# Attention scores of the last row group as three float32r products of split keys and queries

## The chip, the cores and the metric

The kernel runs on one NeuronCore of one Trainium2 chip. The metric is the device time of one execution in microseconds (us), as the median of several executions. A change of less than about 0.2% can hardly be told from none.

TensorE (PE) multiplies matrices and writes to the eight PSUM banks. VectorE (DVE), ScalarE (ACT) and GpSimd (POOL) do the elementwise work, each strictly in the order of its own list of instructions. SyncE (SP) issues nearly all DMAs, also in order. A weight load of PE is shown as a row of its own (PEld).

## The reference

One layer of a token mixer with 2-D neighbourhood attention, between two RMSNorms. x is 2048 tokens x 1024, seen as 32 rows of 64 columns; there are 16 heads of 64.

```
h = rmsnorm(x, norm_0)
q, k, v, gate = split(h @ w_in_0, 4)
# token (r, c) sees 8 rows and 16 columns of keys around it
s = q @ k.T / 8 + bias(rpb_0); s = -1e30 outside the neighbourhood
o = softmax(s) @ v
x = x + (o * silu(gate)) @ w_out_0
out = rmsnorm(x, norm_f)
```

Everything is float32, and the result is compared in float32.

## The kernel before

**Number formats.** A float32 matmul takes several passes over its data. The big products (projections, output projection) avoid them: each operand is split on arrival into a rounded part h and a rest l, both of type float32r, and the product is h·h + h·l + l·h, three matmuls of one pass each. The split is one copy on ACT (it rounds) and one subtraction on DVE. The attention's own products (scores, transposes, values) are plain float32 matmuls.

**Stages.** `stage_one` and `stage_two` compute most of q, k, v and gate and send them to DRAM. Then a loop of 33 iterations does the attention, and PE fills the time between its pieces with the rest of the projections and, later, with the output projection (lines L1346, L1348, L1350, tile `po`), which is handed out in portions by `feed`.

**Attention units.** A unit is a pair of heads p (0 to 7) and a row group T (0 to 3: eight rows of 64 queries each). `order` lists the 32 units: first all p with T = 0, then T = 1 and 2, and at the end, in iterations 24 to 31, all p with T = 3. For T = 3 there are 12 rows of keys, so a tile of keys has 12 x 64 = 768 columns. The two heads of a pair lie in partitions 0 to 63 and 64 to 127 of the tiles `kt` and `q`.

**One iteration m** issues, in this order:

- `begin(m)`: the DMAs for the gate tile `sgt` of unit m-1, the values of unit m, the queries and keys of unit m+1
- a portion of filling work, and then `normalise` of the probabilities of unit m-1 (L1046 and after): a reciprocal on DVE, scalings on POOL and ACT
- `run_roots` (L1248 to L1255: eight small DVE operations for the final norm of an output row block), `split_rows` (L1198, L1199: splits a block for the output projection), the rest of the portion; evacuations of finished `po` banks (L1231 on DVE, then a square on ACT, L1234) and scalings of finished rows (L1263, DVE) come up in between
- `turns(m-1)`: 44 transposes on PE into six banks `ph` (L1112), copied to `pta` by three copies on ACT and three on DVE (L1088)
- `scores(2m)`, `scores(2m+1)`: for each of four column blocks C and both heads s one matmul of 64 x 128 queries by the keys (L1027) into a bank of its own; DVE reads each bank, adds the mask and bias `em` and takes the row's extreme (L1035); ACT takes the exponential (L1041)
- `values(2m-2)`, `values(2m-1)`: matmuls into bank `o` (L1134), which DVE multiplies by `sgt` into `og` (L1140).

All eight PSUM banks are one pool. In an iteration six go to `ph`, eight to the scores, one to `o`, and one holds the unfinished `po`. So the scores take over the banks of `po` and `ph` in turn, each as soon as its copy is done, the last score bank waits for DVE's first read of a score of the same unit, and `o` waits for DVE's second read.

**Portions.** Iterations up to 24 get about 16 matmuls of filling each, iterations 25 to 31 get 53.

```
amount = [dense] * 25
...
amount += [(96 * (12 - len(units_two)) + 546 - sum(amount) - first - end_of_it) / (cycles - 25)] * (cycles - 25) + [end_of_it]
```

Of the kernel before, what the change touches and what calls it, by code (L numbers as in the profile page):

```python
# [10 lines left out]
F32 = mybir.dt.float32  # L11
F32R = mybir.dt.float32r
BF16 = mybir.dt.bfloat16
I32 = mybir.dt.int32
AF = mybir.ActivationFunctionType
OP = mybir.AluOpType
# [4 lines left out]
ROWS, GW, KH, KW = 32, 64, 8, 16  # L21
# [12 lines left out]
KEY_ROWS = [(0, 11), (4, 19), (12, 27), (20, 32)]  # L34
# [36 lines left out]
def build(ctx, tc, x, xr, xt, wg, rpb, last, w_out, n0, nf, masks, out):  # L71
    nc = tc.nc
# [8 lines left out]
    def pool(name, bufs):  # L81
        p = ctx.enter_context(tc.tile_pool(name=name, bufs=bufs))
        return lambda shape, dt, nm: p.tile(shape, dt, name=nm, tag=name)
# [3 lines left out]
    wp = pool("wp", 8)  # L87
    raw = pool("raw", 6)
    kp = pool("kp", 2)
    qp = pool("qp", 2)  # L90
    vp = pool("vp", 2)
    vhalf = []
# [4 lines left out]
            vhalf.extend((t[:, :512], t[:, 512:]))  # L97
        return vhalf.pop(0)

    sp = pool("sp", 2)  # L100
    xp = pool("xp", 8)
    mkp = pool("mkp", 1)
    pt = pool("pt", 1)
    mp = pool("mp", 10)
    ep = pool("ep", 2)

    def sixths():
        t = pt([128, 3072], F32R, "sixths")
        return [t[:, i * 512:i * 512 + 512] for i in range(6)]

    lp = pool("lp", 1)
# [5 lines left out]
    def bank(n, name):  # L117
        return banks.tile([128, n], F32, name=name, tag="bank")
# [138 lines left out]
    for n, (k, j, ph, c) in enumerate(halves):  # L257
        a = (KINDS[k] + j, ph)
# [79 lines left out]
    def must(*keys):  # L338
        assert all(k in written for k in keys), keys
        for n in range(len(later) - 1, -1, -1):  # L340
            if later[n][1] in keys:
                for _ in range(n + 1):
                    later.pop(0)[2]()
                break
# [225 lines left out]
    def stage_one():  # L570
# [6 lines left out]
        land["x12"] = [kp([128, 960], F32, "land")[:, :512] for _ in range(2)] + [xp([128, 512], F32, "land") for _ in range(2)]  # L577
        sixth = sixths()
        land["x21"] = [spot[:, k] for k in range(3)] + [lp([128, 512], F32, "land")]
        slots = [(mp, 512)] * 8 + [(sp, 512)] * 2 + sixth[:2] + [(vh, 512)] * 4  # L580
        slots += sixth[2:] + [(mp, 512)] * 2 + [(qp, 512)] * 2

        def load(f, k):
# [163 lines left out]
        for k in range(4):  # L747
            y = ev([128, 512], F32, "y")
            a, b, c = land["x11"][k], land["x12"][k], land["x22"][k]
# [48 lines left out]
    def stage_two():  # L798
        x12, x11, x21 = L2["x12"], L2["x11"], L2["x21"]
        x22 = [xp([128, 512], F32, "land") for _ in range(4)]  # L800
        sixth = sixths()
        for k in range(4):
            load_x(2, "x22", k, x22[k])
        slots = {"T2": [(mp, 512)] * 8,
                 "T3": [(sp, 512)] * 2 + sixth[:5] + [(lp, 512)],
                 "T4": [(vh, 512)] * 4 + [(mp, 512)] * 2 + [sixth[5], (qp, 512)]}

        def also(n, i):
# [120 lines left out]


    KT, VT, QT, EM, SG, E = {}, {}, {}, {}, {}, {}
    LAST, stored_at = {}, {}
    order = [(p, 0) for p in range(NP)] + [(p, T) for p in range(NP) for T in (1, 2)] + [(p, 3) for p in range(NP)]
    pairs = [(p, T, (h, h + 1)) for p, T in order for h in (0, 2)]
# [9 lines left out]
    def load_k(p, T):  # L944
        r0, r1 = KEY_ROWS[T]
        n = (r1 - r0) * GW
        must(*[("k", p, c) for c in range(r0 // 8, (r1 + 7) // 8)])

        def keys():
            t = kp([128, 960], F32, "kt")  # L950
            KT[p, T] = t.rearrange("p (r c) -> p r c", c=GW)
            nc.sync.dma_start(t[:, :n], kd[p][:, r0 * GW:r1 * GW])

        return keys

    def load_q(p, T):
        must(("q", p, T))
# [58 lines left out]
    def scores(i, between=None):  # L1016
        p, T, cs = pairs[i]
        kt, qt = KT[p, T], QT[p, T]
        r0, r1 = KEY_ROWS[T]
        got = []  # L1020
        for C in cs:
            c0, c1 = KEY_COLS[C]
            qs = slice(C * 128, C * 128 + 128)
            pst = [bank((r1 - r0) * (c1 - c0), f"s{s}") for s in range(2)]
            for s in range(2):
                a = slice(s * 64, s * 64 + 64)
                nc.tensor.matmul(pst[s], qt[a, qs], kt[a, :r1 - r0, c0:c1].rearrange("p r (s c) -> p s r c", c=8), start=True, stop=True)  # L1027
            got.append((C, pst))
        ST[i] = st = tiny.tile([128, 12], F32, name="st")
        for j, (C, pst) in enumerate(got):  # L1030
            n = (r1 - r0) * width(C)
            X[i, C] = [xp([128, 512], F32, f"x{s}")[:, :n] for s in range(2)]
            for s in range(2):
                o = 2 * j + s
                nc.vector.tensor_tensor_reduce(X[i, C][s], pst[s], EM[p, ROW_TYPE[T], COL_TYPE[C], s], -1.0, 1e38,  # L1035
                                               OP.add, OP.min, st[:, o:o + 1])
            if between and j == 0:
                between()
            for s in range(2):
                o = 2 * j + s  # L1040
                nc.scalar.activation(X[i, C][s], X[i, C][s], AF.Exp, bias=st[:, o:o + 1], scale=-1.0,  # L1041
                                     accum_out=st[:, 4 + o:5 + o])

    def normalise(i, both=False, between=None):
        st = ST.pop(i)
        nc.vector.reciprocal(st[:, 8:12], st[:, 4:8])  # L1046
        for j, C in enumerate(pairs[i][2]):
            if j and between:
                between()
            for s in range(2):  # L1050
                o = 8 + 2 * j + s
                if both and j:
                    nc.scalar.activation(X[i, C][s], X[i, C][s], AF.Copy, scale=st[:, o:o + 1])
                else:
                    nc.gpsimd.tensor_scalar(X[i, C][s], X[i, C][s], st[:, o:o + 1], 1.0, op0=OP.mult, op1=OP.mult)  # L1055
# [305 lines left out]
    cycles = len(order)  # L1361
# [14 lines left out]
    def feed(n, calm=0):  # L1376
        credit[0] += n
        while credit[0] > 0 or credit[0] > -calm_debt and clock[0] - state["event"] < calm:
            if alive[0]:
                got = next(fill, None)  # L1380
                if got is None:
                    alive[0] = False
                    continue
            else:
                got = next(outs, None)
                if got is None:
                    due(max(credit[0], 0.0))
                    credit[0] = min(credit[0], 0.0)
                    return
            credit[0] -= got  # L1390
            due(got)
# [37 lines left out]
    for m in range(cycles + 1):  # L1429
        a = amount[m] - 8  # L1430
        begin(m)
        feed(8)
        if m:
            due_here = []
            quiet[0] = True
            if a < 12 and m > 8 and m % 2:
                normalise(2 * m - 1, True, lambda: due_here.append(split_rows() or consume(1, turn=True)))
            else:
                normalise(2 * m - 1, True)
            if a > 12:  # L1440
                run_roots()
            elif not rows_due():
                run_roots(1)
            for k in range(3):
                if m == 1 and k == 2:
                    pass
                elif a > 12 or not any(due_here) and (k < 1 or k < 2 and m > 8 and m % 2 == 0):
                    got = split_rows()
                    due_here.append(got)
                    if not got:  # L1450
                        consume(1, turn=True)
                    elif a < 12 and m % 2 == 0 and len(items) - state["used"] == 8:
                        feed(a * 0.2)
                        consume(1, turn=True)
                feed(a * 0.2)
        else:
            feed(a * 0.6)
        quiet[0] = False
        feed(a * 0.4, 8 if a > 12 else 4)
        sums = next_sums(m) == m + 1  # L1460
        if m:
            turns(m - 1)
            first_sums = m + 2 if m + 2 in pair_steps else m + 1 if sums and m + 1 not in pair_steps else None
            if first_sums:
                after = tiny.tile([128, 12], F32, name="st")
                nc.gpsimd.tensor_scalar(after[:88, 0:1], PT[m - 1][:88, 1, 0:1], ones[:88, 0:1], 1.0, op0=OP.mult, op1=OP.mult)
                tables(first_sums, 0, 1)
        if m == cycles:
            all_loads()
            feed(6)  # L1470
        else:
            scores(2 * m)
            if sums:
                tables(m + 1, 2)
            if m == 0:
                feed(first)
            scores(2 * m + 1, lambda: normalise(2 * m))
            if m == 0:
                consume(2, turn=True)
        if m:  # L1480
            values(2 * m - 2)
            values(2 * m - 1)
        runs[0] += 1
        for n in range(2, 24):
            if n < 8 and m == n - 2 or n == 8 and m == 5 or n in pair_steps and m == n - 3:
                for f in load_e(order[n][0], ROW_TYPE[order[n][1]], homes=accs if n >= 8 and n % 4 == 0 else None):
                    f()
        if m == 20:
            late_loads()
# [52 lines left out]
```

## Time and profile before

| what | value |
|---|---|
| runs | 1056.29, 1057.15, 1058.18 us; median 1057.15 |
| span of the profiled execution, first to last instruction | 1054.4 us |
| what lies around the span, by the median | 2.75 us |
| PE busy | 1046.1 us (99%) |
| DVE, ACT, POOL busy | 696.7, 537.2, 252.0 us |
| granted TensorE clock | 0.999 of full speed |
| iterations with T = 3 scores | scores from 850.3 us to 985.3 us of the span |

The page gives no time for the profiled execution beside its span. PE is busy nearly throughout, so what PE does and what it waits for sets the time. Ends of PE's rows are modelled, and neighbouring matmuls overlap in the rows, so distances between starts say more than durations. Line numbers are those of the kernel before; in the changed kernel the same work stands 18 to 19 lines lower (scores L1045, score reads L1054, copies of the transposes L1107, values L1153, roots L1267, evacuation of `po` L1250).

### The profile page before, as it was taken

Reading aid. Unit: us, or ns where it says so; the run is one execution under the profiler, and the core shown is the slowest. Engines: PE = TensorE matmul, PEld = TensorE weight load, DVE = VectorE, ACT = ScalarE, POOL = GpSimd, SP = SyncE. Lnnn points to the kernel's source line nnn. Section 1 sums busy time; section 2 is a strip of 40 time slices with the busy share of each in tenths; the row PEclk is TensorE's granted clock in tenths of the full one; section 3 lists DMA queues with packets and bytes.
Section 4 is the critical chain, followed back from the end, with each engine's and each line's share of the span. In section 5 each row is a group of like instructions: output and inputs, shape, how many; then the busy total and the mean of one; then the engine's idle time right before and its main releaser. Section 6 shows DMA issues by size and latency. Waiting matters only on the chain.

```text
span 1054.4 us, 20160 instructions
## 1 busy us (share of the span) xinstructions
PE 1046.1 (99%) x7316; PEld 858.8 (81%) x7316; DVE 696.7 (66%) x1570; ACT 537.2 (51%) x1260; POOL 252.0 (24%) x342
## 2 busy tenths in 40 slices
PE   9999999999999999999999999999999999999997
PEld 7888888887888888888888788888887888888886
DVE  5476667778897625555655766687777886667554
ACT  7645223443444334232332677688787865455422
POOL 0000322312211000000002467666665322112100
PEclk9999999999999999999999999999999999999999
DMA  9634444343635433333236777778777588775352
GB/s 320 219 100 118 132 150 136 120 144 120 187 119 154 121 100 93 116 110 121 90 110 211 219 232 235 219 252 281 243 237 217 184 277 272 245 233 183 120 166 80
DMA packets 120252, 184.19 MB, mean 175 GB/s; under 512 B 10776, under 2 KB 55064, under 8 KB 120152
## 3 DMA queue, kind: packets, MB, share of 16 engines
q1 hardware_dynamic: 119720, 182.50, 55.1%
q8 instruction: 57, 0.93, 0.4%
q10 hardware_dynamic: 432, 0.40, 0.1%
q14 instruction: 43, 0.35, 0.1%
HBM read 132.53 MB, written 50.33 MB: 173 GB/s over the span
## 4 chain that ended last, share of the span: by engine, by line
PE 96%; DVE 2%; issue 1%; ACT 1%; DMA 0%; SPq 0%; DVEq 0%; ACTq 0%
PE pp L435 36%; PE pv L559 17%; PE s L1027 8%; PE o L1134 8%; PE po L1346 6%; PE po L1348 5%; PE po L1350 5%; PE ph L1112 4%; PE pp L381 2%; PE pp L383 2%; PE pp L379 2%; DVE f L418 0%; DVE x L1035 0%; DMA raw<-in_wg_dram 0%; DVE raw L424 0%
## 5 line engine op out<-in xcount | busy, mean ns | idle before, releaser
L435 PE MATMUL pp<-h,f 128*128 128x512 f32 x672 | 217.4, 389 | 0.0
L1041 ACT ACTIVATE x<-x,st 128x360 f32<-128x360 f32 (+5 forms) x256 | 151.1, 592 | 23.0 <-DVE st L1035 23.0
L1055 POOL TENSOR_SCALAR x<-x,st 128x480 f32<-128x480 f32 (+5 forms) x192 | 111.7, 599 | 153.5 <-DVE st L1046 148.6
L435 PEld LDWEIGHTS pp<-h,f 128*128 128x128 f32 x672 | 126.2, 188 | 26.2
L435 PE MATMUL pp<-t,f 128*128 128x512 f32 x558 | 141.7, 389 | 0.1
L435 PE MATMUL pp<-l,f 128*128 128x512 f32 x336 | 130.7, 389 | 0.0
L1035 DVE CUSTOM_DVE_ANT_0 x<-s,em 128x360 f32<-128x360 f32 (+5 forms) x256 | 123.0, 535 | 0.5 <-PE s L1027 0.4
L435 PEld LDWEIGHTS pp<-t,f 128*128 128x128 f32 x558 | 104.7, 188 | 22.2 <-DVE u L448 0.6
L455 POOL TENSOR_TENSOR tmp<-tmp,rb 128x512 f32<-128x512 f32 x36 | 58.4, 1622 | 268.3 <-DVE tmp L453 232.8
L995 POOL TENSOR_TENSOR em<-e,mk 128x264 f32<-128x264 f32 (+3 forms) x64 | 50.8, 825 | 259.8 <-PE pp L435 246.3
L418 DVE TENSOR_TENSOR f<-raw,f 128x512 fp32r<-128x512 f32 x105 | 76.5, 729 | 43.6 <-ACT f L417 43.5
L1346 PE MATMUL po<-woh,gh 128*128 128x512 f32 x252 | 99.8, 396 | 0.1
L1348 PE MATMUL po<-woh,gl 128*128 128x512 f32 x252 | 98.7, 391 | 0.0
L1350 PE MATMUL po<-wol,gh 128*128 128x512 f32 x252 | 98.6, 391 | 0.0
L1027 PE MATMUL s<-kt,q 64*128 64x480 f32 (+5 forms) x512 | 94.6, 487 | 0.0
L1134 PEld LDWEIGHTS o<-pta,vt 120*64 120x64 f32 (+2 forms) x1792 | 80.9, 137 | 13.9 <-DVE st L1035 13.6
L559 PE MATMUL pv<-wh,h 128*128 128x512 f32 x256 | 88.3, 390 | 0.0
L559 PE MATMUL pv<-wl,h 128*128 128x512 f32 x256 | 88.2, 390 | 0.2 <-DVE wl L542 0.2
L559 PE MATMUL pv<-wh,l 128*128 128x512 f32 x256 | 88.2, 389 | 0.0
L1088 DVE COPY pta<-ph 120x512 f32<-120x512 f32 (+5 forms) x96 | 56.9, 639 | 43.5 <-PE ph L1112 43.3
L1134 PE MATMUL o<-pta,vt 120*64 120x128 f32 (+5 forms) x1792 | 85.3, 253 | 0.0
L1027 PEld LDWEIGHTS s<-kt,q 64*128 64x128 f32 x512 | 64.9, 186 | 15.3 <-DVE pta L1088 1.3
(156 smaller groups left out, 1705.3 us busy)
## 6 DMA issues: line engine op xcount, KB each, us to landing
raw<-in_wg_dram SPq DMA_DIRECT2D x124, 256.0 KB, 4.3
row<-in_xr_dram SPq DMA_DIRECT2D x32, 256.0 KB, 4.1
vd<-v SPq DMA_DIRECT2D x32, 256.0 KB, 2.5
sgd<-sg SPq DMA_DIRECT2D x32, 256.0 KB, 2.4
q<-qd SPq DMA_DIRECT2D x32, 256.0 KB, 5.2
sgt<-sgd SPq DMA_DIRECT2D x32, 256.0 KB, 4.9
xr<-in_x_dram SPq DMA_DIRECT2D x32, 256.0 KB, 3.8
ogd<-og SPq DMA_DIRECT2D x32, 256.0 KB, 2.7
```

What stands on the lines that cost most here:

```text
L418: nc.vector.tensor_tensor(t[:, 1], src, t[:, 0].bitcast(F32), OP.subtract)
L435: nc.tensor.matmul(B[n, P], t[:, int(m == 2), c], x[k][int(m == 1)], start=P in (1, 6, 5) and k == 0 and m == 0, stop=k == 3 and m == 2, s ...
L455: nc.gpsimd.tensor_tensor(tmp, tmp, rb[c], OP.mult)
L559: nc.tensor.matmul(ps[t], a[:, o], b, start=k == 0 and m == 0, stop=k == NK - 1 and m == 2)
L1027: nc.tensor.matmul(pst[s], qt[a, qs], kt[a, :r1 - r0, c0:c1].rearrange("p r (s c) -> p s r c", c=8), start=True, stop=True)
L1035: nc.vector.tensor_tensor_reduce(X[i, C][s], pst[s], EM[p, ROW_TYPE[T], COL_TYPE[C], s], -1.0, 1e38, OP.add, OP.min, st[:, o:o + 1])
L1041: nc.scalar.activation(X[i, C][s], X[i, C][s], AF.Exp, bias=st[:, o:o + 1], scale=-1.0, accum_out=st[:, 4 + o:5 + o])
L1055: nc.gpsimd.tensor_scalar(X[i, C][s], X[i, C][s], st[:, o:o + 1], 1.0, op0=OP.mult, op1=OP.mult)
L1134: nc.tensor.matmul(to.rearrange("d (h q) -> d h q", q=64) if nq > 64 else to, vt[:k, strip, s * 64:s * 64 + 64], t[:k, h, at:at + 64] if n ...
L1346: nc.tensor.matmul(p, gh, woh[q, j], start=(i == 0), stop=False)
L1348: nc.tensor.matmul(p, gl, woh[q, j], start=False, stop=False)
L1350: nc.tensor.matmul(p, gh, wol[q, j], start=False, stop=(i == NK - 1))
```

## The change

Units with T = 3 split their keys and queries, too. `split_kq` makes a rounded copy `kh` of the keys (ACT, 768 columns) and leaves the rest in `kt` (DVE, in place), then the same for the queries (`qh`, 512 columns). It is called in iterations 24 to 31, right after `normalise` and ahead of `run_roots` and `split_rows`. `scores` then adds three float32r matmuls, `qh`·`kh`, `qh`·`kt`, `q`·`kh`, in each bank, and issues the two heads in turn. The new tile `kh` needs room: the pool of `sgt` shrinks from two buffers to one, and two landing places of the stages move to the new pool.

```
-    sp = pool("sp", 2)
+    sp = pool("sp", 1)
+    khp = pool("khp", 1)
...
-        slots = [(mp, 512)] * 8 + [(sp, 512)] * 2 + sixth[:2] + [(vh, 512)] * 4
+        slots = [(mp, 512)] * 8 + [(sp, 512), (khp, 768)] + sixth[:2] + [(vh, 512)] * 4
...
-                 "T3": [(sp, 512)] * 2 + sixth[:5] + [(lp, 512)],
+                 "T3": [(sp, 512), (khp, 768)] + sixth[:5] + [(lp, 512)],
...
+    KH, QH = {}, {}
+    SPLIT = (3,)
...
+    def split_kq(p, T):
+        n = (KEY_ROWS[T][1] - KEY_ROWS[T][0]) * GW
+        kt, qt = KT[p, T].rearrange("p r c -> p (r c)"), QT[p, T]
+        kh, qh = khp([128, 768], F32R, "kh"), lp([128, 512], F32R, "qh")
+        nc.scalar.activation(kh[:, :n], kt[:, :n], AF.Copy)
+        nc.vector.tensor_tensor(kt[:, :n].bitcast(F32R), kt[:, :n], kh[:, :n].bitcast(F32), OP.subtract)
+        nc.scalar.activation(qh, qt, AF.Copy)
+        nc.vector.tensor_tensor(qt.bitcast(F32R), qt, qh.bitcast(F32), OP.subtract)
+        KH[p, T], QH[p, T] = kh.rearrange("p (r c) -> p r c", c=GW), qh
...
             pst = [bank((r1 - r0) * (c1 - c0), f"s{s}") for s in range(2)]
-            for s in range(2):
-                a = slice(s * 64, s * 64 + 64)
-                nc.tensor.matmul(pst[s], qt[a, qs], kt[a, :r1 - r0, c0:c1].rearrange("p r (s c) -> p s r c", c=8), start=True, stop=True)
+            terms = [(qt, kt)]
+            if T in SPLIT:
+                qh, kh, ql, kl = QH[p, T], KH[p, T], qt.bitcast(F32R), kt.bitcast(F32R)
+                terms = [(qh, kh), (qh, kl), (ql, kh)]
+            for n, (q, k) in enumerate(terms):
+                for s in range(2):
+                    a = slice(s * 64, s * 64 + 64)
+                    nc.tensor.matmul(pst[s], q[a, qs], k[a, :r1 - r0, c0:c1].rearrange("p r (s c) -> p s r c", c=8),
+                                     start=n == 0, stop=n == len(terms) - 1)
...
                 normalise(2 * m - 1, True)
+            if m < cycles and order[m][1] in SPLIT:
+                split_kq(*order[m])
             if a > 12:
                 run_roots()
```

**PE, scores of iteration 24.** Before, a score bank is one float32 matmul. A row ends with the engines (or DMA queues) that it waits for.

```order
L1027 MATMUL s0_9508<-kt_9248,q_9228 128x288 [waits DMAHW7_49,DMAHW6_49,DVE_49]
L1027 MATMUL s1_9509<-kt_9248,q_9228 128x288 [waits Activation_49]
L1027 MATMUL s0_9512<-kt_9248,q_9228 128x384 [waits DVE_49]
L1027 MATMUL s1_9513<-kt_9248,q_9228 128x384 [waits Activation_49]
L1027 MATMUL s0_9529<-kt_9248,q_9228 128x384 [waits DVE_49]
L1027 MATMUL s1_9530<-kt_9248,q_9228 128x384 [waits Activation_49]
L1027 MATMUL s0_9533<-kt_9248,q_9228 128x288 [waits DVE_49]
L1027 MATMUL s1_9534<-kt_9248,q_9228 128x288 [waits DVE_49]
```

And now, for the last two of the four column blocks, with the first matmul of `values` behind them:

```order
L1045 MATMUL s0_9546<-kh_9423,qh_9424 128x384 [waits Activation_49]
L1045 MATMUL s1_9547<-kh_9423,qh_9424 128x384 [waits DVE_49]
L1045 MATMUL s0_9546<-kt_9251,qh_9424 128x384
L1045 MATMUL s1_9547<-kt_9251,qh_9424 128x384
L1045 MATMUL s0_9546<-kh_9423,q_9231 128x384
L1045 MATMUL s1_9547<-kh_9423,q_9231 128x384
L1045 MATMUL s0_9554<-kh_9423,qh_9424 128x288 [waits DVE_49]
L1045 MATMUL s1_9555<-kh_9423,qh_9424 128x288 [waits DVE_49]
L1045 MATMUL s0_9554<-kt_9251,qh_9424 128x288
L1045 MATMUL s1_9555<-kt_9251,qh_9424 128x288
L1045 MATMUL s0_9554<-kh_9423,q_9231 128x288
L1045 MATMUL s1_9555<-kh_9423,q_9231 128x288
```

Three matmuls stand for each one, with s0 (first head) and s1 (second head) in turn; the waits for free banks are where they were. The rest of PE's list is unchanged.

**DVE, iteration 24,** from the reciprocal of `normalise` to the first copy of the transposes, before:

```order
L1046 RECIPROCAL st_9340<-st_9340 128x4
L1248 TENSOR_SCALAR st3_8318<-st3_8318 128x1
...
L1255 TENSOR_SCALAR st3_8318<-st3_8318 128x1
L1231 TENSOR_TENSOR y_9429<-po_9210,xr_8690 128x512
L1263 TENSOR_SCALAR y_8105<-y_8105,st3_8104,acc0_165 128x512
L1263 TENSOR_SCALAR y_8879<-y_8879,st3_8104,acc1_166 128x512
L1088 COPY pta_9451<-ph1_9453 120x512
```

And now:

```order
L1065 RECIPROCAL st_9343<-st_9343 128x4
L964 TENSOR_TENSOR kt_9251<-kt_9251,kh_9423 128x768
L966 TENSOR_TENSOR q_9231<-q_9231,qh_9424 128x512
L1267 TENSOR_SCALAR st3_8321<-st3_8321 128x1
...
L1274 TENSOR_SCALAR st3_8321<-st3_8321 128x1
L1250 TENSOR_TENSOR y_9438<-po_9213,xr_8693 128x512
L1282 TENSOR_SCALAR y_8108<-y_8108,st3_8107,acc0_168 128x512
L1282 TENSOR_SCALAR y_8882<-y_8882,st3_8107,acc1_169 128x512
L1107 COPY pta_9460<-ph1_9462 120x512
```

The two subtractions come in ahead of the roots, the evacuation, the row scalings and the copies of the transposes. On ACT the two rounding copies come in behind the two scalings of `normalise` (L1053) and ahead of the square and ACT's copies of the transposes. Iterations 25 to 31 have the same insertion. The lists of POOL and SP have the same instructions in the same order.

More of the change, by code (lines that the diff above doesn't have):

```diff
@@ L1456, in build @@
         else:
+            if order[0][1] in SPLIT:
+                split_kq(*order[0])
             feed(a * 0.6)
```

## The prediction

> **What bounds the kernel now.** I read the page first, then PE's order of time around one long iteration, then DVE and ACT at the same place, and last the one iteration that differs, 24.
>
> ```profile
> span 1054.4 us, 20160 instructions
> ...
> PE 96%; DVE 2%; issue 1%; ACT 1%; DMA 0%; SPq 0%; DVEq 0%; ACTq 0%
> ...
> L1027 PE MATMUL s<-kt,q 64*128 64x480 f32 (+5 forms) x512 | 94.6, 487 | 0.0
> ```
>
> The chain that ended last is PE for 96%. So PE time saved or lost anywhere goes into the span at its full size, and everything else counts only where PE waits for it. My sum is made against the span and carried to the median, 2.75 us above it.
>
> PE in iteration 26 (columns: start, length, then the work):
>
> ```profile
> 875.05 0.39 PE L1348 MATMUL po<-woh,gl 128*128 128x512 f32 x1
> ...
> 886.88 0.39 PE L1350 MATMUL po<-wol,gh 128*128 128x512 f32 x1
> 887.20 1.43 PE L1112 MATMUL ph<-ident,x 64*96 64x64 f32 x44
> 888.47 2.73 PE L1027 MATMUL s<-kt,q 64*128 64x288 f32 x16
> 891.12 2.67 PE L1134 MATMUL o<-pta,vt 96*64 96x128 f32 x56
> ```
>
> Between the first two rows lie 52 steps of float32r matmuls: 11.83/52 = 0.2275 us for 512 columns, 0.444 ns a column. The scores have 8 float32 matmuls in 16 records, which start at 888.47; values follow at 891.12, 2.65 us later. Four matmuls have 288 columns and four 384, 2688 in all.
>
> Do the two heads share the array? The weight loads of the second head's last three records of 384 columns follow its matmuls' starts; ACT's second copy of the transposes stands with them:
>
> ```profile
> 889.15 0.18 PEld L1027 LDWEIGHTS s<-kt,q 64*128 64x128 f32 x1
> ...
> 889.58 0.19 PEld L1027 LDWEIGHTS s<-kt,q 64*128 64x128 f32 x1
> 889.91 0.19 PEld L1027 LDWEIGHTS s<-kt,q 64*128 64x128 f32 x1
> 890.23 0.19 PEld L1027 LDWEIGHTS s<-kt,q 64*128 64x128 f32 x1
> ...
> 888.51 0.59 ACT L1088 ACTIVATE pta<-ph 96x512 f32<-96x512 f32 x1
> ```
>
> A head's records come 0.325 us apart. By the column price above one pass of 384 columns is 0.17 us, so a record is two passes (0.42 ns a column and pass), and a float32 matmul four. Sixteen records alone would take 4 x 2688 x 0.42 = 4.5 us; the group takes 2.65. The two heads run beside each other, 2.26 us each, and no room for the 0.19 us of a weight load is left in 0.325: loads hide. The row at 889.15 starts 0.05 us after that copy on ACT ends (889.10); it is the fourth bank, freed by that copy.
>
> **The change part by part.**
>
> *Scores, iterations 26 to 31.* The fourth bank stays where it is, 889.15, since the copy does not move. From there to `values` the second head has three matmuls (384 + 384 + 288 = 1056 columns). Before: 4 passes x 1056 x 0.42 = 1.77 us, and 0.2 us for the first load and the change to `values`, which is the measured 1.97. After: 3 passes, at 0.42 ns 1.33 us, at the 0.444 of the float32r row 1.41 us. The saving is 0.36 to 0.44 us; I take 0.37, since the 0.444 row has the same number format. Before 889.15 nothing is gained, because the bank decides. Six iterations: -2.2 us. That float32r matmuls of 64 partitions share the array as float32 ones do is shown by no row; the other end is rival A.
>
> One rule of the Trainium skill speaks against this. "TensorE: Matmul & The Clock Gate", Part 3, "The mechanism", says that a weight load overlaps running matmuls only when its row group differs, so each head's loads would stand between its own matmuls. By the float32 rows here it does not hold (0.325 us for two passes of 384); by the rule, the sum would be that of rival B instead of mine.
>
> *Splits, iteration 24.* This iteration still has a short portion, and DVE has no gap:
>
> ```profile
> 846.43 0.18 DVE L1248 TENSOR_SCALAR st<-st 128x1 f32<-128x1 f32 x1
> ...
> 848.56 0.69 DVE L1231 TENSOR_TENSOR y<-po,xr 128x512 f32<-128x512 f32 x1
> ...
> 850.49 1.75 DVE L1088 COPY pta<-ph 120x512 f32<-120x512 f32 x3
> 852.15 0.45 DVE L1035 CUSTOM_DVE_ANT_0 x<-s,em 128x288 f32<-128x288 f32 x1
> ...
> 850.32 3.10 PE L1027 MATMUL s<-kt,q 64*128 64x288 f32 x16
> 853.35 2.67 PE L1134 MATMUL o<-pta,vt 120*64 120x128 f32 x56
> ...
> PEld s L1027 <- DVE pta L1088: 0.7, 2, 0.4
> ...
> PEld o L1134 <- DVE st L1035: 0.4, 1, 0.4
> ```
>
> Here the scores take 3.03 us, and the two waits show why: the banks come free by DVE's copies and reads, already late. What is put into DVE ahead of them goes to PE in full. Prices and place of the four instructions:
>
> ```profile
> 846.55 1.09 ACT L1053 ACTIVATE x<-x,st 128x360 f32<-128x360 f32 x2 [0.25 <-DVE st L1046]
> ...
> L417 ACT ACTIVATE f<-s x42: 614/632/632, 89.8 to 559.1; 128x512 fp32r<-128x512 f32 x42
> L418 DVE TENSOR_TENSOR f<-s,f x42: 671/684/1785, 90.5 to 561.1; 128x512 fp32r<-128x512 f32 x42
> ...
> 1038.59 0.21 DVE L1248 TENSOR_SCALAR st<-st 128x1 f32<-128x1 f32 x1 [0.84 <-ACT xr L1234]
> ...
> 1040.31 0.75 DVE L1263 SCALAR_TENSOR_TENSOR y<-y,st,acc 128x512 f32<-128x512 f32 x1
> ```
>
> `kh` starts on ACT when L1053 is done, at 847.6. 512 columns take 0.63 us, so 768 take between 0.63 and 0.95; with a fixed part, about 0.8: done at 848.4. DVE, free at 846.43, waits for it, about 2.0 us. The first subtraction is between 0.68 and 1.03 us, say 0.9 in a row of work; the second adds 0.6 to 0.7. The roots begin at about 849.9 instead of 846.43: 3.45 us late. Of that some comes back: the eight roots take 2.13 us here (846.43 to 848.56), beside POOL's scalings, and 1.72 us at 1038.59 to 1040.31, where POOL is idle; at 849.9 POOL has finished too. So DVE's copies and reads come 3.0 to 3.45 us late, I take 3.1. ACT's copies wait behind the square, which waits for L1231, and are as late. After DVE's first read the last score bank needs three passes of 288 columns instead of four, 0.1 us less. Iteration 24: +3.0 us (least, with only the two subtractions' 1.5 us and no waiting: +1.4; most +3.4).
>
> *Splits, iteration 25.* The delay is the same 3 us, and the idle time ahead of the copies about as long:
>
> ```profile
> 860.65 1.29 DVE L1199 TENSOR_TENSOR gl<-ograw,gh 128x512 fp32r<-128x512 f32 x2
> ...
> 865.59 0.69 DVE L1231 TENSOR_TENSOR y<-po,xr 128x512 f32<-128x512 f32 x1 [0.44 <-PE po L1350]
> 868.92 0.69 DVE L1088 COPY pta<-ph 96x512 f32<-96x512 f32 x1 [2.64 <-PE ph L1112]
> ...
> 866.31 0.63 ACT L1234 ACTIVATE xr<-y 128x512 f32<-128x512 f32 x1 [1.97 <-DVE y L1231]
> ...
> 865.62 0.39 PE L1348 MATMUL po<-woh,gl 128*128 128x512 f32 x1
> ```
>
> 0.44 + 2.64 = 3.1 us of idle takes up DVE's delay. ACT's square waits for L1231, now near 868.7, and holds ACT's copies 0.3 to 0.4 us; that eats the gain of 0.37. Iteration 25: 0. The split at 860.65, whose `gl` PE first uses at 865.62, ends its first half at about 864.3: still in time.
>
> *Iterations 26 to 31* have the room:
>
> ```profile
> DVE pta L1088 <- PE ph L1112: 20.6, 6, 5.1
> DVE y L1231 <- PE po L1350: 13.8, 7, 3.4
> ```
>
> 34.4 us of idle in six iterations, 5.7 each, against 3.1. Late evacuations hold one PSUM bank more, but between two attention pieces the others are free. Cost: 0.
>
> *One buffer for `sgt`.* Its DMA now waits for the previous `og` on DVE:
>
> ```profile
> DMA to landing us min/median/max: 3.2/4.9/7.5
> ...
> 700.78 0.69 DVE L1140 TENSOR_TENSOR og<-o,sgt 128x512 f32<-128x512 f32 x1
> ...
> 711.45 0.69 DVE L1140 TENSOR_TENSOR og<-o,sgt 128x512 f32<-128x512 f32 x1 [0.37 <-PE o L1134]
> ```
>
> Free at 701.5, landed by 709.5 at the slowest, used at 711.45. SP's next instruction there, the store of that same `og`, waits for the same end, so what is queued behind (values, queries, keys) moves by one issue, about half a us, and is used an iteration later. Cost: 0. The landing places in the stages keep their sizes in use and order: 0.
>
> **Sum:** +3.0 + 0 - 2.2 = +0.8 us on 1054.4 of span, so about 1058.0 us by the median, 0.08% over it: inside the 0.2% (2.1 us) that a measurement tells from no change.
>
> **The rivals.**
>
> *A, slower: the heads do not share the array in float32r.* For it: no row shows float32r on 64 partitions. Against it: the float32 rows share it. Price: 3 x 2688 x 0.444 = 3.58 us for a group, plus 0.2, against 2.65: +1.1 in seven iterations and about +3.3 in iteration 24: +11 us, 1068. It decides from the moment a head's record waits for the other's.
>
> *B, slower: weight loads are not hidden.* Nine records follow the fourth bank; each would add 0.1 to 0.19 us (the recorded 0.19 is an upper end): +0.9 to +1.7, less 0.37, in seven iterations, and +3.3: +7 to +12.6 us, 1064 to 1070. For it: single passes of 0.13 to 0.17 us give a load less cover than 0.325. Against it: the rows above.
>
> *C, faster: DVE's lateness in iteration 24 does not reach PE.* Then seven gains remain: -2.6 us, 1054.6. Against it: the two waits of PE for DVE in that very group.
>
> **How the numbers follow.** My sum's own range is -1.0 (iteration 24 at its least, gains at 0.44) to +2.0 (gains at 0.3, iteration 24 at its most, something lost in 25): 1056.1 to 1059.2. Chances: forecast 0.62 within 0.2%, 0.09 that the same mechanism ends over +2.1 us because float32r records cost more than 0.444 or a later iteration runs short too; A 0.12; B 0.12; C 0.05. So faster 0.05, same 0.62, slower 0.33. The range takes in the lower half of B: 1055.6 to 1064.0; outside remain A, the upper part of B and some of C, about 0.2.
>
> **What would show it.** In the changed trace: score groups of 24 records at L1045; from their start to `values` about 2.3 us in iterations 26 to 31 (3.8 would be A, over 3 B); in iteration 24 a group of about 6 us, with PE's weight loads waiting for DVE's L1107 and L1054; DVE idle about 2 us between the reciprocal and L964 there; roots then in about 1.7 us. The prediction is wrong if that group is near 3 us (C), or if `og` waits for `sgt`.

## The result and the profile after

| | median us | runs |
|---|---|---|
| before, in the same runs | 1056.83 | 1056.14 to 1058.97 |
| after | 1058.93 | 1058.35 to 1060.42 |
| ratio after/before | 1.0021, 95% interval 1.0012 to 1.0030 | |

The change costs about 2.1 us (2.2 by the ratio), 0.21% with an interval from 0.12% to 0.30%. That lies inside the predicted range; whether it is over or under the 0.2% that the forecast expected it to stay under can't be told. The profiled execution of the changed kernel is one of its longer ones: 1060.42 us, a span of 1058.6. Its page, the lines that answer to those of before:

```profile
span 1058.6 us, 20339 instructions
...
PE 1048.3 (99%) x7380; PEld 863.6 (82%) x7380; DVE 705.0 (67%) x1586; ACT 546.8 (52%) x1276; POOL 251.9 (24%) x342
```

PE is busy 2.2 us more, and the span is 4.2 us longer. Where that is, PE's, DVE's and ACT's order of time in iteration 24 show (start, length, work, and in brackets the idle time before it with its releaser):

```profile
849.89 1.51 PE L1131 MATMUL ph<-ident,x 64*120 64x64 f32 x44
853.21 0.39 PE L1045 MATMUL s<-kh,qh 64*128 64x288 f32 x1 [1.81 <-DVE y L1250]
854.36 0.60 PE L1045 MATMUL s<-kh,qh 64*128 64x288 f32 x1 [0.76 <-ACT pta L1107]
...
855.97 0.75 PE L1045 MATMUL s<-kh,qh 64*128 64x384 f32 x2
856.29 0.75 PE L1045 MATMUL s<-kt,qh 64*128 64x384 f32 x2
...
858.01 3.73 PE L1153 MATMUL o<-pta,vt 120*64 120x128 f32 x56
861.67 0.50 PE L1367 MATMUL po<-woh,gl 128*128 128x512 f32 x1
...
847.25 0.18 DVE L1065 RECIPROCAL st<-st 128x4 f32<-128x4 f32 x1 [0.40 <-ACT x L1060]
849.31 0.96 DVE L964 TENSOR_TENSOR kt<-kt,kh 128x768 fp32r<-128x768 f32 x1 [1.89 <-DMA ogd<-og]
850.19 0.68 DVE L966 TENSOR_TENSOR q<-q,qh 128x512 fp32r<-128x512 f32 x1
850.79 0.21 DVE L1267 TENSOR_SCALAR st<-st 128x1 f32<-128x1 f32 x1
...
852.38 0.69 DVE L1250 TENSOR_TENSOR y<-po,xr 128x512 f32<-128x512 f32 x1
852.98 1.41 DVE L1282 SCALAR_TENSOR_TENSOR y<-y,st,acc 128x512 f32<-128x512 f32 x2
854.30 1.75 DVE L1107 COPY pta<-ph 120x512 f32<-120x512 f32 x3
...
848.45 0.83 ACT L963 ACTIVATE kh<-kt 128x768 fp32r<-128x768 f32 x1
...
853.10 0.63 ACT L1253 ACTIVATE xr<-y 128x512 f32<-128x512 f32 x1 [3.30 <-DVE y L1250]
```

DVE stands for 1.89 us ahead of its first subtraction. The named releaser, a DMA, is not it: the subtraction starts 0.03 us after ACT's rounding copy (848.45 + 0.83) ends. Then the roots start 3.5 us after the reciprocal, and DVE's copies of the transposes at 854.30, against 850.49 before; less the 0.9 us by which the two executions are apart when the transposes start, 2.9 us late. PE has done its transposes at about 851.4 (849.89 + 1.51) and waits 1.81 us for the evacuation L1250, whose bank the first score takes over, then 0.76 us for ACT's copy of the transposes. What the prediction did not have is in PE's last rows: records of 384 columns are 0.32 us apart, against 0.19 in iteration 27 (below), and `values` take 3.5 us, against 2.44 before. The clock, by stretches of time (transposes with the idle time, scores, values; the number before the last two is the granted clock):

```profile
849.89:853.21 3.32, 1.51 (x45) 1.40 (x45) 3.08 (x12) 0.11 (x1) 0.00 (x0) 1.00 0.79 192
853.21:858.01 4.80, 4.04 (x24) 3.53 (x24) 4.80 (x14) 3.52 (x10) 0.00 (x0) 0.52 1.04 321
858.01:861.52 3.51, 3.51 (x55) 3.51 (x56) 1.66 (x9) 3.02 (x12) 2.11 (x4) 0.68 0.98 378
```

I call the time from the first transposes to the last of `values` the piece of iteration 24: 11.63 us here (849.89 to 861.52). Before, in one row:

```profile
848.98:855.79 6.81, 6.81 (x117) 5.48 (x116) 6.68 (x22) 5.22 (x16) 0.42 (x1) 1.00 0.93 267
```

So +4.8 us. Some of it comes back later. Iteration 27 of the changed kernel, PE, its weight loads and ACT (`x2`: one record of each head):

```profile
912.63 0.50 PE L1045 MATMUL s<-kh,qh 64*128 64x288 f32 x2
...
913.83 0.53 PE L1045 MATMUL s<-kh,qh 64*128 64x384 f32 x2
914.02 0.53 PE L1045 MATMUL s<-kt,qh 64*128 64x384 f32 x2
...
915.12 0.44 PE L1153 MATMUL o<-pta,vt 96*64 96x128 f32 x4
...
913.34 0.18 PEld L1045 LDWEIGHTS s<-kh,qh 64*128 64x128 f32 x1
...
912.07 1.22 ACT L1107 ACTIVATE pta<-ph 96x512 f32<-96x512 f32 x2 [1.67 <-PE ph L1131]
```

From the first score to `values` it is 2.49 us (before 2.65). The fourth bank still comes free with ACT's second copy, which ends at 912.07 + 1.22 = 913.29; the load at 913.34 is the first for it. From that load to `values` it is 1.78 us, against 1.97 before. A head's records of 384 columns are 0.19 us apart, and both heads run in that time. From the transposes of iteration 26 to those of iteration 31 the changed kernel takes 93.30 us (892.77 to 986.07), the one before 94.12 (887.20 to 981.32): 0.16 us gained in each iteration, where 0.37 was predicted.

### The profile page after: what moved, and what is told of

Its sections match the earlier page's. It is cut to its first block, busy times and chain, and to the rows that moved or that the text cites. A ratio compares the mean times of both kernels' runs of the same rounds, so it can differ in the third digit from the quotient of the medians.

```text
span 1058.6 us, 20339 instructions
## 1 busy us (share of the span) xinstructions
PE 1048.3 (99%) x7380; PEld 863.6 (82%) x7380; DVE 705.0 (67%) x1586; ACT 546.8 (52%) x1276; POOL 251.9 (24%) x342
## 5 line engine op out<-in xcount | busy, mean ns | idle before, releaser
L1054 DVE CUSTOM_DVE_ANT_0 x<-s,em 128x360 f32<-128x360 f32 (+5 forms) x256 | 123.0, 535 | 0.2 <-PE s L1045 0.2
L1107 DVE COPY pta<-ph 120x512 f32<-120x512 f32 (+5 forms) x96 | 56.9, 639 | 35.0 <-PE ph L1131 34.8
L418 ACT ACTIVATE f<-raw 128x512 fp32r<-128x512 f32 x105 | 63.7, 624 | 26.5 <-PE pp L436 12.5
L436 PEld LDWEIGHTS pp<-l,f 128*128 128x128 f32 x336 | 63.1, 188 | 13.2
```

Of the source, the lines that this page charges most:

```text
L418: nc.scalar.activation(t[:, 0], src, AF.Copy)
L436: nc.tensor.matmul(B[n, P], t[:, int(m == 2), c], x[k][int(m == 1)], start=P in (1, 6, 5) and k == 0 and m == 0, stop=k == 3 and m == 2, s ...
```

## The experiments

All against the kernel before, with runs of it on the same chip. "Piece" is that of iteration 24, "group" the time from the first score to `values` in iteration 27, both in the profiled execution.

| kernel | median us (before) | ratio, 95% interval | piece | group |
|---|---|---|---|---|
| before | | | 6.81 | 2.65 |
| changed | 1058.93 (1056.83) | 1.0021, 1.0012 to 1.0030 | 11.63 | 2.49 |
| again | 1059.34 (1056.81) | 1.0023, 1.0014 to 1.0032 | 10.56 | 2.49 |
| not24 | 1055.42 (1056.46) | 0.9988, 0.9980 to 0.9997 | 6.80 | 2.50 |
| only24 | 1059.97 (1056.46) | 1.0030, 1.0019 to 1.0042 | 11.75 | 2.66 |
| onebuf | 1056.71 (1056.46) | 1.0001, 0.9992 to 1.0010 | 6.81 | 2.65 |
| room24 | 1058.47 (1056.46) | 1.0017, 1.0008 to 1.0026 | 7.80 | 2.49 |
| late24 | 1056.78 (1056.60) | 1.0003, 0.9995 to 1.0012 | 8.23 | 2.54 |
| pool24 | 1057.58 (1056.67) | 1.0012, 1.0003 to 1.0020 | 8.91 | 2.52 |
| warm24 | 1058.57 (1056.81) | 1.0015, 1.0006 to 1.0024 | 9.64 | 2.51 |
| bf16 | 1056.44 (1056.60) | 0.9995, 0.9986 to 1.0005 | 10.00 | 2.12 |
| bf16not24 | 1052.81 (1056.67) | 0.9968, 0.9956 to 0.9980 | 6.81 | 2.12 |
| apart | 1060.66 (1056.60), one run | | 10.63 | 2.50 |
| two | 1056.15 (1056.60), one run | | 10.42 | 2.18 |

The intervals are about 1 us to each side, so differences of less are read from the pieces, not from the medians.

### Where the time is lost: iteration 24 left out, and alone

```
-            if T in SPLIT:                                    (both, in scores)
+            if (p, T) in QH:
...
-            if m < cycles and order[m][1] in SPLIT:
+            if 24 < m < cycles and order[m][1] in SPLIT:      (not24)
+            if m == 24:                                       (only24)
```

> Keys and queries are split in iterations 25 to 31 only; iteration 24 keeps its float32 scores and the plain order on DVE. Theory 1 (the prediction's sizes: +3.0 us in iteration 24, a gain of 0.37 us in six iterations): without iteration 24 only the gains stay, -2.2 us, or -2.6 if iteration 25 gains too. Theory 2 (sizes read from the changed kernel's trace: score groups of 2.49 to 2.52 us instead of 2.65, transposes 0.03 us shorter, so 0.16 to 0.19 us in seven iterations): -1.1 to -1.3 us. Rival (the added microsecond comes from elsewhere, from the single buffer of sgt or from the later stores): no faster than before. Iteration 24 has 16 score records, 3.0 us from their start to values, and no drop of the clock.

> Keys and queries are split in iteration 24 only; iterations 25 to 31 keep float32 scores. Theory 1 (DVE's lateness goes into PE): +3.0 us (bounds +1.4 to +3.4). Theory 2 (the same lateness, and PE, idle for about 3 us ahead of the scores, runs the group and a part of values at about half clock): between +3.2 us where the clock holds and +4.8 us where it drops, with records of 384 columns 0.32 us apart in the second case. Rival (iteration 24 is not where the time is lost): within 1 us of before. With the run that leaves iteration 24 out, the two should add up to the whole change, about +2.1 us.

Without iteration 24 the kernel is faster than before, by 1.0 us (1.3 by the ratio); with it alone it is slower by 3.5 (3.2 by the ratio). The two add up to 2.5 (1.9 by the ratios), and the whole change costs 2.1 to 2.5. In `not24` theory 2 holds and theory 1 has the gains too large. In `only24` the time does not tell the two apart, since 3.0 lies inside the interval too; the trace does. The granted clock is down as in the changed kernel, 0.65 in `values` and 0.55 in the scores, which are this row:

```profile
852.55:857.35 4.80, 4.02 (x25) 3.53 (x25) 4.80 (x14) 3.52 (x10) 0.00 (x0) 0.55 1.04 336
```

The kernel without iteration 24 also shows what iteration 25 costs. There, in order of time:

```profile
869.00 1.43 PE L1131 MATMUL ph<-ident,x 64*96 64x64 f32 x44
870.25 0.39 PE L1045 MATMUL s<-kh,qh 64*128 64x288 f32 x1
870.80 0.40 PE L1045 MATMUL s<-kh,qh 64*128 64x288 f32 x1 [0.16 <-ACT pta L1107]
...
869.54 0.63 ACT L1253 ACTIVATE xr<-y 128x512 f32<-128x512 f32 x1 [1.44 <-DVE y L1250]
```

ACT's square waits for DVE and holds ACT's copies; the group there takes 2.84 us instead of 2.65. In the changed kernel the same group takes 2.52, because PE itself arrives late and DVE has caught up.

### The single buffer

```
-    SPLIT = (3,)
+    SPLIT = ()
```

> Nothing is split; what is left of the change is the one buffer for sgt in place of two, the new pool, and the two landing places. Theories 1 and 2: 0 us, within 0.5, and og waits for PE alone. Rival (the single buffer delays gate tiles, or the queue behind them): +1 us or more, with og waiting for a DMA.

No difference can be told (1.0001), and in the list of waits `og` waits for PE alone:

```profile
DVE og L1159 <- PE o L1153: 12.4, 29, 1.2
```

### More PE work ahead of the late engines

```
+    amount[25] -= 14
...
+        if m == 24:
+            feed(14)
```

> The whole change, and 14 matmuls of filling work move from iteration 25 to iteration 24, between its portion and the transposes (14 x 0.2275 = 3.2 us of PE work). Theory 2: in iteration 24 DVE and ACT catch up behind these matmuls, so PE neither waits nor loses clock there, and only the gains stay: -1.1 to -1.4 us against before. Theory 1 gives -2.2 to -2.6 us. Rival (the lateness comes back in iteration 25, whose own room shrinks by 3.2 us, or the moved matmuls bring evacuations that DVE has to do first): the time stays above before, at +1 us or more.

The rival held: +2.0 us. The clock stays up and the piece is down to 7.80 us, but the rest turns up elsewhere. In this kernel's order of time:

```profile
856.22 0.46 PE L1045 MATMUL s<-kh,qh 64*128 64x384 f32 x2 [1.25 <-DVE pta L1107]
...
868.74 0.50 PE L1367 MATMUL po<-woh,gl 128*128 128x512 f32 x1 [1.24 <-DVE gl L1218]
...
852.83 2.73 DVE L1282 SCALAR_TENSOR_TENSOR y<-y,st,acc 128x512 f32<-128x512 f32 x4
```

DVE now has four row scalings in iteration 24 instead of two; and in iteration 25 PE reaches the next `gl` before DVE has split it, 1.24 us, and the scores there take 3.28 us. So here moving PE's work moved the place where PE waits.

### The two subtractions later on DVE

```
-        nc.vector.tensor_tensor(kt..., kt, kh, OP.subtract)    (and that of q)
+        def rests(): (both subtractions)
...
+                if m > 24:
+                    rests()                                  (where they were)
...
+        if m == 24:
+            rests()
         if m:
             turns(m - 1)
```

> The whole change, but in iteration 24 DVE's two subtractions stand behind its roots, evacuation and row scalings, right ahead of its copies of the transposes; ACT's rounding copies stay where they are. If 2 of the 3 us are DVE's waiting for ACT's copy (1.9 us in the changed kernel's rows), DVE no longer waits and its copies come late by the subtractions alone, about 1.5 us; ACT's own copies of the transposes are not late; PE loses 1.2 to 1.6 us there, no clock drop, and with 0.16 to 0.19 us gained in seven iterations the time is +0.1 to +0.4 us against before. Rival (the work itself, or ACT, makes the lateness): still +2 us or more.

As theory: 1.0003, and the piece is 1.42 us longer than before. Its DVE goes through without waiting, and the copies come at 852.41:

```profile
849.62 1.40 DVE L1286 SCALAR_TENSOR_TENSOR y<-y,st,acc 128x512 f32<-128x512 f32 x2
850.94 0.95 DVE L968 TENSOR_TENSOR kt<-kt,kh 128x768 fp32r<-128x768 f32 x1
851.81 0.68 DVE L969 TENSOR_TENSOR q<-q,qh 128x512 fp32r<-128x512 f32 x1
```

So of the 2.8 us that iteration 24 loses with the clock kept up (`warm24`, below) half is waiting for ACT's copy and half the work.

### The two subtractions on POOL

```
+        eng = nc.gpsimd if (p, T) == order[24] else nc.vector      (both subtractions are then on eng)
```

> The whole change, but in iteration 24 POOL does the two subtractions, behind its scalings. If it is DVE's list that makes PE late, DVE's roots, evacuation and copies are as early as before, the scores start when the transposes end, and PE waits only for POOL's rest of the keys and queries: POOL is free at about 849 us, and by its rows (360 columns of a scaling 0.64 us, 512 of a product of two tiles 1.62 us) the two take 2.3 to 4.0 us, so that the third product waits up to 2 us. Against before: -1.0 to +0.8 us, no clock drop. Rival (ACT's copies make the lateness, or POOL slows DVE down as much): +2 us or more.

+0.9 us (1.3 by the ratio), between the theories: the piece is 2.10 us longer than before, the clock stays up. PE does not wait for POOL's results, but once more for the evacuation (here L1251) and for the copies, since DVE is held in another way:

```profile
848.69 1.82 POOL L965 TENSOR_TENSOR kt<-kt,kh 128x768 fp32r<-128x768 f32 x1 [0.46 <-ACT kh L963]
...
848.53 0.16 DVE L1274 SCALAR_TENSOR_TENSOR st<-st 128x1 f32<-128x1 f32 x1
848.73 1.81 DVE L1275 SCALAR_TENSOR_TENSOR st<-st 128x1 f32<-128x1 f32 x1
```

A root operation on one column, 0.16 us otherwise, lasts until POOL's subtraction ends.

### The clock

```
+            again = 2 if m == 23 and b else 0       (the second half of the transposes three times)
```

> The changed kernel once more, on the chip of the next run and beside it. As before: about 2 us over the kernel before; executions with a mean granted clock of 0.995 to 0.996 lie 1 to 2 us above those with 0.997 to 0.999, since the clock drops in iteration 24 in all of them, for a shorter or a longer time.

> The whole change, and in iteration 24 the second half of the transposes is done three times over into the same banks, 44 more transposes, 1.24 us of work by the rows, in the 1.8 us in which PE stands idle there; nothing reads a bank before the last pass. If PE's idle time is what takes the clock down, it stays at full speed, the scores and values of iteration 24 get 1 to 2.5 us shorter and the time is 1 to 2 us under the changed kernel's, although more is done; against before 0 to +1 us. If the clock drops for another reason, or if the added work itself is on the path, the time is as the changed kernel's or up to 1.2 us more.

In `again`, the changed kernel once more, the same idle time is there (3.32 us from the first transposes to the scores), but the clock drops later and comes back sooner; with the repeated transposes it does not drop. First `again`, then `warm24`, by the same three stretches:

```profile
850.15:853.47 3.32, 1.51 (x45) 1.40 (x45) 3.08 (x12) 0.11 (x1) 0.00 (x0) 1.00 0.81 198
853.47:858.23 4.76, 3.99 (x24) 3.49 (x24) 4.76 (x14) 3.48 (x10) 0.00 (x0) 0.65 1.03 325
858.23:860.71 2.48, 2.48 (x57) 2.48 (x56) 1.70 (x9) 2.48 (x11) 1.27 (x3) 0.98 1.04 403
```

```profile
849.13:852.46 3.33, 2.92 (x89) 2.81 (x89) 3.09 (x12) 0.11 (x1) 0.00 (x0) 1.00 0.85 216
852.46:856.33 3.87, 3.09 (x25) 2.21 (x25) 3.87 (x10) 2.59 (x8) 0.00 (x0) 1.00 1.03 310
856.33:858.77 2.44, 2.44 (x56) 2.44 (x56) 2.31 (x12) 2.44 (x10) 0.34 (x1) 1.00 1.02 403
```

The scores start just as late (3.33 us after the transposes), so DVE's lateness is untouched, and yet the piece is 9.64 us instead of 10.56 and 11.63. PE's idle time takes the clock down, and the drop costs the piece 0.9 to 2.0 us. In the median little of it is left, 0.8 us where 1 to 2 were expected, and that within the intervals: with PE less late, iteration 25 has less time (its group takes 2.94 us, in `again` 2.52). So that the drop costs the whole kernel something is shown by the pieces, not by the medians. That executions of lower mean clock are 1 to 2 us longer held only in part: eleven runs of `again` gave 1058.94 to 1060.32 at 0.995 and 0.996, and 1057.84 to 1059.64 at 0.998 and 0.999.

### The price of a record

> The three products take their parts in bfloat16 instead of float32r (the parts are smaller, so the rounding of the scores changes), the places are the same. If the 30 ns that each record of a head takes over its columns at 2.4 GHz belong to float32r, records of 384 columns come 0.16 to 0.17 us apart, values start about 0.07 us earlier in iterations 26 to 31, and the time is 0.4 to 0.6 us under the changed kernel's. If they belong to the 64-row tiles or to the two heads in turn, the pitch stays 0.19 us and the time within 0.3 us of the changed kernel's.

> The three products of one head stand together, then those of the other; nothing else. If two heads run beside each other only when their records alternate, a group of iterations 26 to 31 takes nearly the sum of its 24 records: 12 x 0.19 + 12 x 0.15 less overlaps at the changes, 3.3 to 4.1 us instead of 2.49, and the time is 5 to 10 us over the changed kernel's. If PE looks further ahead than three records, the group stays at 2.5 to 2.7 us.

> The third product (the rest of the queries by the rounded keys) is left out in the last row group, so the scores are less exact. It prices one product behind the fourth bank: by theory 1 (0.444 ns a column) the group of iterations 26 to 31 gets shorter by 0.17 + 0.17 + 0.13 = 0.47 us, by theory 2 (30 ns a record more) by 0.19 + 0.19 + 0.15 = 0.53 us, to 1.96 us. Rival (the time from the fourth bank to values is set by DVE's reads of the scores, not by PE's records): shorter by 0.3 us at most.

```
-                for s in range(2):                             (apart: the loops exchanged)
+            for s in range(2):
+                for n, (q, k) in enumerate(terms):
...
-                terms = [(qh, kh), (qh, kl), (ql, kh)]
+                terms = [(qh, kh), (qh, kl)]                   (two)
...
-        kh, qh = khp([128, 768], F32R, "kh"), lp([128, 512], F32R, "qh")
+        kk, qq = khp([128, 1536], BF16, "kh"), lp([128, 1024], BF16, "qh")   (bf16)
```

In `apart` the group stays at 2.50 us: PE starts the other head's records though three of the first stand ahead of them. Whether the heads alternate in the code doesn't matter. (The single time of 1060.66 is no price of that: its piece of iteration 24 is 10.63 us, between those of the changed kernel's two profiles, and its transposes there start 1.5 us later than in the changed kernel's profile, ahead of the edit.)

In `two` the group is 2.18 us, 0.31 less than with three products, not 0.47 or 0.53; that is the rival, and the run gives no price of a record. There the last bank waits for DVE's first read of the scores:

```profile
911.77 0.41 PE L1045 MATMUL s<-kh,qh 64*128 64x288 f32 x1
...
911.26 0.44 DVE L1054 CUSTOM_DVE_ANT_0 x<-s,em 128x288 f32<-128x288 f32 x1
```

That is the next bound, 0.3 us from the changed kernel's state.

In `bf16` the group is 2.12 us, and the time 2.3 us under the changed kernel's by the medians' distances to before (2.7 under `again`); the expectation of 0.07 and 0.5 us counted three records behind the fourth bank where there are nine, and is far too small. The weight loads are half as long, too. The loads grouped by form, and the order of time in iteration 27:

```profile
L1046 PEld LDWEIGHTS s<-kt,q x384: 182/187/191, 585.2 to 843.1; 64*128 64x128 f32 x192
...
L1046 PEld LDWEIGHTS <-qh x192: 92/94/148, 851.5 to 985.6; 64*128 64x128 bf16 x192
```

```profile
910.64 2.19 PE L1046 MATMUL s<-kh,qh 64*128 64x288 bf16 x24
912.75 0.33 PE L1154 MATMUL o<-pta,vt 96*64 96x128 f32 x2
...
911.32 1.19 PEld L1046 LDWEIGHTS <-qh 64*128 64x128 bf16 x16 [0.29 <-issue]
```

From the fourth bank (911.32) to `values` it is 1.43 us, in float32r 1.78, in float32 1.97. In the half-clock rows 384 columns take 0.32 us, 0.83 ns a column, so 0.417 at full clock; in `bf16` the second head's records of 384 columns behind the fourth bank start 0.162 us apart (911.32, 911.48, 911.64 and so on), which is nearly the same. The second head's 3 x 1056 columns are 1.32 us. From the fourth bank on `bf16` takes that and 0.1; float32r that, 0.2 for its start, and nine times 0.03. So the 64 rows and the two heads alone do not make the 0.03 us a record; it takes float32r. But float32r alone does not make it either: the output projection's records of 512 columns on 128 rows take 0.2275 us, 0.014 over their 512 x 0.417. Whether the 0.03 is the matmul's or a rest of the weight load, which is twice as long, that is not hidden, these runs don't separate.

### A version that beats both

> The parts in bfloat16 (so the rounding of the scores changes), split in iterations 25 to 31 only. With groups of 2.12 us (2.65 before) and no late DVE in iteration 24, seven gains of 0.5 us, less what iteration 25 gives back (about 0.3 us): -3.0 to -3.7 us against before. Rival (the values that now start sooner wait for DVE or for their DMA, or the filling work takes the gain back): no more than -1.5 us.

bfloat16 parts, split in iterations 25 to 31 only: 1052.81 us, 3.9 under before, 3.4 by the ratio (0.9968, 0.9956 to 0.9980), as expected. Six groups of 2.12 us and one of 2.45 (iteration 25) instead of 2.65 make 3.4. Its scores are rounded differently from those of the changed kernel.

## Why the prediction came out as it did

*Splits, iteration 24: right in cause and place, wrong in the wait, short by the clock.* It said +3.0 us through DVE's lateness, with DVE idle for 2.0 us ahead of the first subtraction (1.89), the first subtraction 0.9 (0.96) and roots in 1.7 us (1.6). With the clock kept up (`warm24`) the piece is 2.8 us longer. The wait was not the one it named, of PE's weight loads for DVE's L1107 and L1054: L1250 held PE ahead of the group, and ACT's L1107 behind the group's first record. So the group is 4.80 us long (3.87 in `warm24`), not about 6, and the rest of the lateness stands between the first transposes and the scores, 3.32 us against 1.34 before. Missing from the sum was a term for what PE's own idle time does: the clock at half, 0.9 to 2.0 us more in the two profiles. The prediction had the idle time in hand and put no price on it.

The Trainium skill ("TensorE: Matmul & The Clock Gate", Part 1, "What's actually happening") puts the return to half clock "after ≥1 idle window (~3.4µs)". Here the measurement differs: the clock fell 2.0 us after the last transposes, with one record in between, as the windows show:

```profile
851.40:853.40 2.00, 0.19 (x1) 0.18 (x1) 1.85 (x7) 0.30 (x1) 0.00 (x0) 1.00 0.82 206
853.40:859.90 6.50, 5.74 (x44) 5.26 (x45) 6.27 (x22) 5.22 (x17) 0.72 (x2) 0.50 1.03 345
```

It was back at about 860.3. In `again` it fell near 854.9, 3.3 us after them, with one record in between, too, which comes nearer to the rule, and was back at about 858.3:

```profile
854.50:855.00 0.50, 0.39 (x4) 0.39 (x5) 0.50 (x2) 0.50 (x3) 0.00 (x0) 0.93 0.95 201
...
858.00:858.50 0.50, 0.50 (x7) 0.27 (x6) 0.50 (x5) 0.50 (x3) 0.00 (x0) 0.66 1.06 420
```

Gaps of 1.25 us (`room24`) and of 0.55 and 0.78 us (`pool24`) left it at 1.00. By windows of 0.1 us the clock stood at half for 6.83 us in the changed kernel and in `only24`, and for 3.41 us in `again`, `bf16` and `two`: the one time is twice the other, and no length in between occurred in these five.

*Scores, iterations 26 to 31: the place right, the size wrong.* The fourth bank, freed by ACT's copy, does decide, and only the second head's nine records behind it count. The term that was mis-sized is "at the 0.444 of the float32r row 1.41 us": it measured 1.58 (1.78 less the 0.20 for the first load and the change to `values`). 0.444 ns a column came from records of 512 columns on 128 rows, 0.014 us each over their columns' time. The price per column hides this part, but by it nine records would still take only 1.45 us; the records here have about twice as much, 0.03. With it the saving comes out at 0.18 (measured 0.19), and the iterations gave 0.16 each: -1.0 us, not -2.2.

*Splits, iteration 25: 0.* In the changed kernel its group takes 2.52 us, a gain as in the others. But the reason given, that the square's wait for L1231 eats the gain, is right where PE is on time, and there it eats more than the gain: 2.84 and 2.94 us in `not24` and `warm24`, against 2.65 before.

*The single buffer and the landing places, iterations 26 to 31's room for DVE: 0.* Right (`onebuf`, groups of 2.49 us).

*The sum.* +3.0 - 2.2 = +0.8 was forecast; by the profiles it is 2.8 + (0.9 to 2.0) - 7 x 0.16, +2.6 to +3.7, and the medians say +2.1 to +2.5, with 1 us to each side. Both misses go the same way: a gain half as large, and a cost that was not in the sum. The range that the sum had of its own ended at +2.0 us, so the result lies at or over its edge (its lower end, by the way, should be -1.2: 1.4 less six times 0.44). That the time lies well inside the stated range is luck, since the upper end of that was set by a rival that did not occur. The 0.09 given to an end over +2.1 us named one of the two causes, records that cost more than 0.444 a column; the clock stood nowhere.

*The rivals.* A fell: 0.19 us for a pair of records of both heads. B fell: its price of 0.1 us or more a record would show as a pitch of at least 0.26, and it is 0.19; a load that is not hidden by 0.03 us is not excluded. So the rule of the Trainium skill that the prediction cited for it, on weight loads and row groups, does not hold here for loads in the same row group. C fell with `only24`.

## What to carry to other kernels

Ahead of a stage in which PE already waits for DVE, an instruction costs its own time and also its wait for the producer. Put the producer's half early and the consumer's half where its input is long done; here that took the loss of the piece from 2.8 us, with the clock kept up, to 1.4. A time per column from long records hides a fixed part: price short records by the record, from rows of the same shape. And a stall of PE can have a second price, the clock afterwards: here gaps of 1.81 and 0.76 us with one record in between had it, a gap of 1.25 us did not.

## What was not expected of the hardware

- The clock fell to 0.50 after 2.0 us with nearly no PE work, stayed there for 6.8 us in one execution and for 3.4 us in another of the same kernel; 44 useless transposes in the gap kept it up.
- A float32r record of 384 columns on 64 rows takes 0.19 us at full clock, 0.03 more than in bfloat16 (0.162). At half clock it takes 0.32, twice the bfloat16 time, so that nothing over the columns' time shows there.
- While POOL subtracts two tiles (1.82 us), a DVE operation of one column with two tensor inputs takes 1.81 us instead of 0.16. The Trainium skill ("GPSIMD Engine Reference", 8. Key points) has POOL sharing its SBUF interfaces with VectorE, in contention with instructions of two SBUF inputs; the rows agree, and here the one waits for the whole of the other.
